# Float32r weights of a hybrid layer: two fixed tiles of four quarters in place of four rotating buffers

## The chip, the cores and the metric

The kernel runs on one core of a Trainium2 chip. The metric is the device time of one execution of the program, in microseconds (us). The engines are named as in the profile: PE is TensorE's matrix multiplication and PEld its loading of weights, DVE is VectorE, ACT is ScalarE, POOL is GpSimd, and SP is the engine that issues most of the DMAs here. SBUF is the on-chip memory that the engines read; an address below is a byte offset within one of its 128 partitions.

## The reference

One layer of an encoder with attention and convolution, for 512 frames of a new stream and 64 frames of a running one (576 in all), with 2048 features:

```python
def hybrid_layer(x, k_past, v_past, conv_past, g_norm1, w_in, g_q, g_k, conv_w,
                 g_attn_out, g_conv_out, w_out, g_norm2, w_gate, w_up, w_down):
    ...
    hn = rmsnorm(x, g_norm1)
    proj = hn @ w_in
    q, k, v, gb, gc, hc = jnp.split(proj, ...)
    ...
    o_attn = stick_breaking_blocks(q, k_all, v_all, P).reshape(B, T, ATTN_W)
    u = gc * hc
    padded = jnp.concatenate([conv_past.astype(u.dtype), u], axis=1)
    conv = (conv_w[0] * padded[:, 0:T] + conv_w[1] * padded[:, 1:T + 1]
            + conv_w[2] * padded[:, 2:T + 2])
    o_conv = gb * conv
    ...
    mix = jnp.concatenate([rmsnorm(o_attn, g_attn_out), rmsnorm(o_conv, g_conv_out)], axis=-1)
    x = x + mix @ w_out
    h2 = rmsnorm(x, g_norm2)
    x = x + (jax.nn.silu(h2 @ w_gate) * (h2 @ w_up)) @ w_down
    return x, k, v, new_conv
```

There are 8 heads of 128 for the attention and 8 groups of 128 channels for the convolution; `w_in` has 6144 columns, `w_out` 2048, `w_gate` and `w_up` 5632 each, and `w_down` has 5632 rows. Everything is float32. Nearly all of the arithmetic is in the five matrix products.

## The kernel before, in words

**How a float32 product is made.** TensorE multiplies in the type float32r, which keeps fewer bits than float32. Each operand is therefore split in two: the high part is a cast to float32r (on ACT), the low part is the operand minus its high part (on DVE). A product is then the sum of three matmuls: high weights by high frames, low weights by high frames, high weights by low frames. These three matmuls of one 128x128 weight block with 288 frames (half of 576) stand one behind the other in the program; the prediction calls them a triple. So the weight operand alternates high, low, high.

**Columns.** Part of the input projection and the whole output projection go column by column. A column is 2048 elements of each partition: 16 weight blocks of 128 columns for `w_in`, 8 blocks of 256 columns for `w_out`. A DMA brings the raw column (`load_weight`), `weight_split` takes the two tiles for its parts, and ACT and DVE fill them in halves of 1024 elements (`weight_parts`, L211). `step` (L301) issues the three matmuls and `product` the whole column. There are 20 such columns of `w_in`, 4 early ones, 10 late ones beside the attention and 6 for the convolution, and 8 of `w_out` (`out_proj`). Raw columns are loaded and split ahead of their use by small generators that the matmul stream advances (`Pipeline.tick`).

**Units.** The rest of the input projection and all of the feed-forward part use units: 2x2 blocks multiplied with seven products instead of eight (Strassen's way, in a form with sums of frames and of weights). A product of a unit is 24 matmuls on a weight operand of 1024 elements (8 weight blocks by three), or fewer in the down projection and in some units of the convolution. `unit_weights` takes a tile for high and low part of such an operand: the low part at the tile's start, the high part from element 1040. A `prepare` function casts and subtracts some products ahead (L310, L311 in the gate, up and down units), and a `multiply` function issues the matmuls: L1181 in the first units, L1534 in the units of the convolution, L2047 in gate, up and down.

**The buffers.** The weight pool has three tags: `raw` (one tile), `whi` and `wlo`, with two buffers each. Each tile of the last two has 2064 elements, 8256 bytes. A column takes the next `whi` buffer for its high part and the next `wlo` buffer for its low part. A unit's product takes one buffer, from `whi` and `wlo` in turn, for both its parts. In the built program the buffers start at bytes 19200 and 27456 (`whi`), 35712 and 43968 (`wlo`).

**The order.** The order of TensorE's instructions is written out by hand for the whole program. Those of ACT, DVE, POOL and SP are set by a scheduler up to the last gate unit but one, SP's in parts by hand, and by hand behind that. In the output projection (L1727 and L1728 multiply the finished PSUM tile and add it to the residual) the DVE order is thus the scheduler's.

Of the kernel before, what the change touches and what calls it, by code (L numbers as in the profile page):

```python
# [11 lines left out]
F32R = mybir.dt.float32r  # L12
# [4 lines left out]
P = 128  # L17
# [50 lines left out]
def down_calls():  # L68

    done, calls, gone = [0] * DC, [], 0  # L70
    for d, a, b in DOWN:
        assert done[d] == a and b <= gone + SLOTS
        done[d] = b
        calls.append([p + SLOTS for p in range(gone, min(done)) if p + SLOTS < NFP])
        gone = min(done)
    assert gone == NFP
    return calls


class TwoParts:  # L80

    def __init__(self, hi, lo):
        self.two = (hi, lo)

    def __getitem__(self, key):
        part, rest = key[1], (key[0], *key[2:])
        if isinstance(part, slice):
            return TwoParts(*(t[rest] for t in self.two[part]))
        return self.two[part][rest]
# [31 lines left out]
def tile_hybrid_stream_step(  # L121
# [6 lines left out]
    nc = tc.nc  # L128
# [12 lines left out]
    wpool = ctx.enter_context(tc.tile_pool(name="wpool", bufs=2, side="left"))  # L141
# [34 lines left out]
    first_out = len(specs)  # L176
# [9 lines left out]

    ready = []
    raw_tile = {"A": wpool.tile([P, 2, 2048], F32, tag="raw", name="raw_a", bufs=1)}

    def weight_tile(tag, name):  # L190
        return wpool.tile([P, 2064], F32R, tag=tag, name=name)[:, :2048]

    def unit_weights(turn):
        t = wpool.tile([P, 2064], F32R, tag=("whi", "wlo")[turn % 2], name="whl")
        return TwoParts(*(t[:, a : a + 1024].rearrange("p (j c) -> p j c", c=P) for a in (1040, 0)))

    def weight_raw(i):
        src, nk, ncol = specs[i]
# [2 lines left out]

    def weight_split(i):
        nk, ncol = specs[i][1:]
        hi = weight_tile("whi", f"whi{i}")[:, : nk * ncol]
        lo = weight_tile("wlo", f"wlo{i}")[:, : nk * ncol]
        ready.append((hi.rearrange("p (k c) -> p k c", k=nk), lo.rearrange("p (k c) -> p k c", k=nk)))
        return hi, lo

    def weight_parts(raw, hi, lo, a, b, lo_eng):
        nc.scalar.copy(out=hi[:, a:b], in_=raw[:, a:b])  # L210
        lo_eng.tensor_tensor(out=lo[:, a:b], in0=raw[:, a:b], in1=hi[:, a:b].bitcast(F32), op=ALU.subtract)  # L211

    raws = {}
# [6 lines left out]
    def split_weight(lo_eng):  # L220
        raw = raws[len(ready)]
        n = specs[len(ready)][1] * specs[len(ready)][2]
        hi, lo = weight_split(len(ready))
        for a in range(0, n, 1024):
            weight_parts(raw, hi, lo, a, a + 1024, lo_eng)
# [255 lines left out]
    with tc.manual_schedule(engines={mybir.EngineType.Activation, mybir.EngineType.DVE, mybir.EngineType.SP}):  # L481
        raw, raw3, src = weight_raw(0)
        raws[0] = raw
        hi, lo = weight_split(0)
# [873 lines left out]
    def load_sum(q, j0=None):  # L1358
        if not j0:
            bt[q] = bt["pool"].tile([P, NP, 2, HALF], F32R, tag=f"t{q}", name=f"xs_t{q}")  # L1360
        j0, j1 = (0, NP) if j0 is None else (j0, j0 + 4)
        nc.sync.dma_start(out=bt[q][:, j0:j1].bitcast(F32), in_=xs_dram[q, j0:j1].rearrange("j f p t -> p j f t"))
# [248 lines left out]
    def load_forms(tile_, at, f):  # L1611
        ft[f] = tile_[:, at : at + NH // 2]
        nc.sync.dma_start(out=ft[f].bitcast(F32), in_=form_dram[f - 1].rearrange("j f p t -> p j f t"))
# [23 lines left out]
    def add_x(d):  # L1637
        nc.gpsimd.dma_start(out=x2t[d], in_=xt_dram[2 * d : 2 * d + 2].rearrange("k p t -> p k t"), accum_op=ALU.add)
# [26 lines left out]
    corder = [(0, 1), (0, 2), (1, 1), (0, 7), (0, 6), (1, 2), (0, 5), (0, 3), (0, 4), (1, 6), (1, 7), (1, 5)]  # L1665
# [17 lines left out]
    for k_, (n, p_) in enumerate(corder):  # L1683
        if (n, p_) == (NCU - 1, 1):
            turn_mode.enter_context(tc.manual_schedule(engines={mybir.EngineType.SP}))
        if k_ == len(begin) - 1:
            start_mode.close()
        conv_run(n, p_)
        for q in begin[k_] if k_ < len(begin) else range(k_ + 4, min(k_ + 5, len(corder))):
            conv_prepare(*corder[q])  # L1690
        if k_ in (0, 2):
            load_sum(3, k_ * 2)
        if n == NCU - 1 and p_ in (6, 7, 4):
            q = {6: 1, 7: 2, 4: 3}[p_]
            t = bt["pool"].tile([P, NH, 2, HALF], F32R, tag=f"t{q}", name=f"forms{q}")
            for at, f in enumerate({1: (1, 2), 2: (6, 7), 3: (5, 3)}[q]):
                load_forms(t, 4 * at, f)
            if p_ == 7:
                load_forms(apool.tile([P, NH // 2, 2, HALF], F32R, tag="oa", name="forms0"), 0, 4)
        if (n, p_) == (NCU - 1, 3):  # L1700
            open_out()
        if n >= NCU and p_ == (3 if n < NCU + 2 or n == len(CU) - 1 else 4):
            add_x(n - NCU)
        if k_ in (len(corder) - 10, len(corder) - 5):
            load_weight()
        if k_ == len(corder) - 4:
            split_weight(nc.vector)

    turn_mode.close()

# [437 lines left out]
    turn = [0]  # L2148
# [252 lines left out]
```

## Time and profile before

| | us |
|---|---|
| median of 3 runs | 2323.15 (2323.01 to 2323.67) |
| the profiled execution | 2322.45 |
| its span, first to last instruction | 2320.7 |

The mean granted clock of TensorE was 0.999. The stages follow one another on TensorE, with the share of the window that each kept TensorE busy, from the windows view of the whole kernel:

| stage | window, us | PE busy | matmuls |
|---|---|---|---|
| start, early columns | 0 to 62 | 59.35 | 432 |
| first units | 62 to 182 | 119.75 | 909 |
| attention, late columns, columns of the convolution | 182 to 455 | 272.43 | 2018 |
| units of the convolution | 455 to 745 | 289.74 | 2194 |
| output projection | 745 to 846 | 101.00 | 768 |
| gate and up units | 846 to 1834 | 987.33 | 7481 |
| down units | 1834 to 2320.7 | 481.00 | 3649 |

In the rows quoted below, a line such as `PE MATMUL psy<-h_s,whl 128*128 128x288 f32 x21` is a run of 21 matmuls into the PSUM tile `psy`, with the frames of tile `h_s` and the weights of tile `whl`, of 128x128 weights and 128x288 frames. L2047 is the line of the kernel. The busy length of a row overlaps the next row's start, because matmuls are pipelined; what a product takes is read from start to start. In the windows view a row holds the window, its length, and then busy time and count for PE and PEld, the granted clock, the busy share of the DMA engines and GB/s.

### The profile page before, as it was taken

Reading aid. Unit: us, or ns where it says so; the run is one execution under the profiler, and the core shown is the slowest. Engines: PE = TensorE matmul, PEld = TensorE weight load, DVE = VectorE, ACT = ScalarE, POOL = GpSimd, SP = SyncE. Lnnn points to the kernel's source line nnn. Section 1 sums busy time; section 2 is a strip of 40 time slices with the busy share of each in tenths; the row PEclk is TensorE's granted clock in tenths of the full one; section 3 lists DMA queues with packets and bytes.
Section 4 is the critical chain, followed back from the end, with each engine's and each line's share of the span. In section 5 each row is a group of like instructions: output and inputs, shape, how many; then the busy total and the mean of one; then the engine's idle time right before and its main releaser. Section 6 shows DMA issues by size and latency. Waiting matters only on the chain.

```text
span 2320.7 us, 43744 instructions
## 1 busy us (share of the span) xinstructions
PE 2310.6 (100%) x17437; PEld 2302.8 (99%) x17437; DVE 1919.7 (83%) x2853; ACT 1161.1 (50%) x2016; POOL 285.3 (12%) x394
## 2 busy tenths in 40 slices
PE   9999999999999999999999999999999999999999
PEld 9999999999999999999999999999999999999999
DVE  8977887888877899888888888888888777887886
ACT  7535887444455564444444444444444444444444
POOL 2002343111111210000000000000000001431121
PEclk9999999999999999999999999999999999999999
DMA  8776554953389454543544444444344936886543
GB/s 278 214 205 166 154 155 107 345 190 109 107 278 248 145 166 145 160 153 122 155 139 141 150 135 150 133 146 156 114 156 143 357 111 223 223 230 203 195 125 107
DMA packets 584869, 402.54 MB, mean 173 GB/s; under 512 B 91870, under 2 KB 571864, under 8 KB 584664
## 3 DMA queue, kind: packets, MB, share of 16 engines
q1 hardware_dynamic: 574136, 378.56, 52.3%
q0 software_dynamic: 10160, 20.94, 4.0%
q8 instruction: 136, 2.23, 0.4%
q14 instruction: 69, 0.57, 0.1%
q10 hardware_dynamic: 368, 0.24, 0.0%
HBM read 303.53 MB, written 96.16 MB: 172 GB/s over the span
## 4 chain that ended last, share of the span: by engine, by line
PE 88%; DVE 6%; DMA 2%; SPq 2%; issue 1%; ACT 1%; POOL 0%; ACTq 0%; DVEq 0%
PE psy L2047 34%; PE psw L2047 17%; PE psx L2047 8%; PE pj L301 8%; PE psy L1534 7%; PE psw L1534 3%; PE psy L1181 3%; PE psx L1534 2%; PE psw L1181 1%; PE psx L1181 1%; DMA raw_a<-in_w_in_dram 1%; SPq L2244 1%; DMA raw_b<-in_w_down_dram 1%; DVE whl L311 1%; DVE wlo L211 1%
## 5 line engine op out<-in xcount | busy, mean ns | idle before, releaser
L2047 PE MATMUL psy<-h_s,whl 128*128 128x288 f32 x2787 | 410.6, 294 | 0.0
L2047 PEld LDWEIGHTS psy<-h_s,whl 128*128 128x128 f32 x2787 | 382.5, 188 | 0.0
L311 DVE TENSOR_TENSOR whl<-raw_a,whl 128x1024 fp32r<-128x1024 f32 (+4 forms) x296 | 318.2, 1076 | 54.8 <-ACT whl L310 53.6
L2047 PE MATMUL psw<-t,whl 128*128 128x288 f32 x2400 | 346.9, 295 | 0.0
L2047 PEld LDWEIGHTS psw<-t,whl 128*128 128x128 f32 x2400 | 326.9, 188 | 0.2 <-DVE whl L311 0.2
L310 ACT CAST whl<-raw_a 128x1024 fp32r<-128x1024 f32 (+4 forms) x296 | 267.6, 906 | 103.8 <-issue 35.3
L301 PE MATMUL pj<-x,whi 128*128 128x288 f32 x1248 | 272.6, 299 | 0.1
L311 DVE TENSOR_TENSOR whl<-raw_b,whl 128x1024 fp32r<-128x1024 f32 (+5 forms) x190 | 198.9, 1047 | 66.1 <-ACT whl L310 65.0
L310 ACT CAST whl<-raw_b 128x1024 fp32r<-128x1024 f32 (+5 forms) x190 | 165.1, 871 | 166.5 <-issue 72.3
L2057 ACT COPY part<-psy 128x288 f32<-128x288 f32 x242 | 96.3, 398 | 277.9 <-PE psy L2047 275.7
L301 PEld LDWEIGHTS pj<-x,whi 128*128 128x128 f32 x1248 | 207.4, 189 | 0.8 <-DVE x L464 0.3
L301 PE MATMUL pj<-x,wlo 128*128 128x288 f32 x624 | 184.1, 295 | 0.0
L2047 PE MATMUL psy<-t2t,whl 128*128 128x288 f32 x1212 | 182.9, 294 | 0.0
L2047 PE MATMUL psy<-b22m,whl 128*128 128x288 f32 x1212 | 182.7, 294 | 0.0
L2047 PE MATMUL psx<-h_s,whl 128*128 128x288 f32 x1185 | 173.1, 294 | 0.0
L2047 PEld LDWEIGHTS psy<-t2t,whl 128*128 128x128 f32 x1212 | 167.8, 188 | 0.3 <-DVE whl L311 0.3
L2047 PEld LDWEIGHTS psy<-b22m,whl 128*128 128x128 f32 x1212 | 167.7, 188 | 0.0
L2047 PEld LDWEIGHTS psx<-h_s,whl 128*128 128x128 f32 x1185 | 162.2, 188 | 0.0
L310 ACT CAST whl<-s 128x1024 fp32r<-128x1024 f32 (+5 forms) x81 | 72.2, 891 | 98.5 <-PE psw L2047 98.5
L1826 POOL DMA_DIRECT2D hid_dram<-form x3 | 2.3, 752 | 968.9 <-DVE form L311 967.7
L301 PEld LDWEIGHTS pj<-x,wlo 128*128 128x128 f32 x624 | 117.7, 189 | 0.4
L2047 PE MATMUL psy<-t,whl 128*128 128x288 f32 x576 | 106.8, 295 | 1.3 <-ACT part L2057 1.3
(535 smaller groups left out, 4550.9 us busy)
## 6 DMA issues: line engine op xcount, KB each, us to landing
hid_dram<-form SPq DMA_DIRECT2D x147, 288.0 KB, 2.2
raw_a<-in_w_in_dram SPq DMA_DIRECT2D x31, 1024.0 KB, 5.5
raw_a<-in_w_gate_dram SPq DMA_DIRECT2D x22, 1024.0 KB, 5.4
raw_a<-in_w_up_dram SPq DMA_DIRECT2D x22, 1024.0 KB, 5.6
raw_b<-in_w_gate_dram SPq DMA_DIRECT2D x22, 1024.0 KB, 6.6
raw_b<-in_w_up_dram SPq DMA_DIRECT2D x22, 1024.0 KB, 6.4
h_s<-hid_dram SPq DMA_DIRECT2D x10, 2016.0 KB, 11.9
raw_a<-in_w_out_dram SPq DMA_DIRECT2D x16, 1024.0 KB, 5.5
```

Of the source, the lines that this page charges most:

```text
L211: lo_eng.tensor_tensor(out=lo[:, a:b], in0=raw[:, a:b], in1=hi[:, a:b].bitcast(F32), op=ALU.subtract)
L301: mm(ps, w_[:, k, csl], x_, start=(k == 0 and n == 0), stop=(k == nk - 1 and n == 2))
L310: nc.scalar.copy(out=hi, in_=src)
L311: (lo_eng or nc.vector).tensor_tensor(out=lo, in0=src, in1=hi.bitcast(F32), op=ALU.subtract)
L1181: mm(ps, whl[:, w_, j, :], x_, start=(start and j == 0 and q == 0), stop=(j == NP - 1 and q == 2), skip_group_check=True)
L1534: mm(ps, whl[:, w_, j, :], x_, start=(start and j == 0 and q == 0), stop=(j == m - 1 and q == 2), skip_group_check=True)
L1826: q.dma_start(out=hid_dram[fp][2 * n - 2 : 2 * n].rearrange("f p t -> p f t"), in_=t.bitcast(F32))
L2047: mm(ps, whl[:, w_, j, :], x_, start=(start and j == 0 and q == 0), stop=(j == len(xs_) - 1 and q == 2), skip_group_check=True)
L2057: nc.scalar.copy(out=t, in_=st["y"])
L2244: nc.sync.dma_start(out=y[g : g + t1 - t0, b0 : b0 + 32].rearrange("(b t) c -> t b c", t=32), in_=ap[32 * q : 32 * (q + 1), t0:t1].rearran ...
```

## The change

`whi` and `wlo` become two fixed tiles with one buffer each: `low_all` of 4096 elements and `high_all` of 4160, with four quarters of 1024 elements each (those of `high_all` start at element 16). The bytes of both together are the same as those of the four buffers. `quarter` hands out the quarters in a ring: a unit's product takes one, with its high part in `high_all` and its low part in `low_all`; a column takes two, and `Halves` indexes the two as one. In the built program `low_all` starts at byte 19200 and `high_all` at 35584. The split of the first output column is written as two halves, one product of the convolution apart, instead of one call.

```diff
--- before.py
+++ after.py
@@ -77,6 +77,19 @@
     return calls
 
 
+class Halves:
+
+    def __init__(self, parts, size):
+        self.parts, self.size = parts, size
+
+    def __getitem__(self, key):
+        i = key[1]
+        half = ((i.start or 0) if isinstance(i, slice) else i) // self.size
+        off = half * self.size
+        i = slice((i.start or 0) - off, i.stop - off) if isinstance(i, slice) else i - off
+        return self.parts[half][(key[0], i, *key[2:])]
+
+
 class TwoParts:
 
     def __init__(self, hi, lo):
@@ -186,13 +199,18 @@
 
     ready = []
     raw_tile = {"A": wpool.tile([P, 2, 2048], F32, tag="raw", name="raw_a", bufs=1)}
-
-    def weight_tile(tag, name):
-        return wpool.tile([P, 2064], F32R, tag=tag, name=name)[:, :2048]
+    low_all = wpool.tile([P, 4096], F32R, tag="wlo", name="low_all", bufs=1)
+    high_all = wpool.tile([P, 4160], F32R, tag="whi", name="high_all", bufs=1)
+    ring = [0]
+
+    def quarter():
+        a = ring[0] % 4
+        ring[0] += 1
+        b = 16 + a * 1024
+        return high_all[:, b : b + 1024], low_all[:, a * 1024 : a * 1024 + 1024]
 
     def unit_weights(turn):
-        t = wpool.tile([P, 2064], F32R, tag=("whi", "wlo")[turn % 2], name="whl")
-        return TwoParts(*(t[:, a : a + 1024].rearrange("p (j c) -> p j c", c=P) for a in (1040, 0)))
+        return TwoParts(*(t.rearrange("p (j c) -> p j c", c=P) for t in quarter()))
 
     def weight_raw(i):
         src, nk, ncol = specs[i]
@@ -201,10 +219,10 @@
 
     def weight_split(i):
         nk, ncol = specs[i][1:]
-        hi = weight_tile("whi", f"whi{i}")[:, : nk * ncol]
-        lo = weight_tile("wlo", f"wlo{i}")[:, : nk * ncol]
-        ready.append((hi.rearrange("p (k c) -> p k c", k=nk), lo.rearrange("p (k c) -> p k c", k=nk)))
-        return hi, lo
+        assert nk * ncol == 2048
+        two = list(zip(quarter(), quarter()))
+        ready.append(tuple(Halves([t.rearrange("p (k c) -> p k c", c=ncol) for t in part], nk // 2) for part in two))
+        return tuple(Halves(part, 1024) for part in two)
 
     def weight_parts(raw, hi, lo, a, b, lo_eng):
         nc.scalar.copy(out=hi[:, a:b], in_=raw[:, a:b])
@@ -1704,7 +1722,10 @@
         if k_ in (len(corder) - 10, len(corder) - 5):
             load_weight()
         if k_ == len(corder) - 4:
-            split_weight(nc.vector)
+            first_split = weight_split(first_out)
+            weight_parts(raws[first_out], *first_split, 0, 1024, nc.vector)
+        if k_ == len(corder) - 3:
+            weight_parts(raws[first_out], *first_split, 1024, 2048, nc.vector)
 
     turn_mode.close()
 
```

TensorE's and POOL's rows are the same as before, one for one, apart from the names of the weight tiles. The orders that a scheduler makes of ACT, DVE and SP differ in a few stretches at the end of the convolution's units and in the output projection. Two of them follow.

The first is DVE in the output projection, in the fourth column. `low_all<-raw_a,high_all` (before: `wlo<-raw_a,whi`) is the subtraction that makes a low part for a coming column, `po<-pjo,R_c` the multiply that empties a PSUM tile of a finished product, and `x_3` a block of the residual; `h_s` and `b` are operands of the feed-forward part. Before:

```order
L1727 TENSOR_TENSOR po<-pjo,R_c 128x288
L1728 TENSOR_TENSOR x_3_7946<-po,x_3_7946 128x288
L1776 SCALAR_TENSOR_TENSOR h_s_8998<-x_3_7946,vec,h_s_8998 128x288
L1727 TENSOR_TENSOR po<-pjo,R_c 128x288
L1728 TENSOR_TENSOR x_3_7946<-po,x_3_7946 128x288
L211 TENSOR_TENSOR wlo_9631<-raw_a,whi_9630 128x1024 x2
L1776 SCALAR_TENSOR_TENSOR b_9621<-x_3_7946,vec,b_9621 128x288
```

Of the change:

```order
L1748 TENSOR_TENSOR po<-pjo,R_c 128x288
L1749 TENSOR_TENSOR x_3_7806<-po,x_3_7806 128x288
L1797 SCALAR_TENSOR_TENSOR h_s_8804<-x_3_7806,vec,h_s_8804 128x288
L229 TENSOR_TENSOR low_all<-raw_a,high_all 128x1024
L1748 TENSOR_TENSOR po<-pjo,R_c 128x288
L229 TENSOR_TENSOR low_all<-raw_a,high_all 128x1024
L1749 TENSOR_TENSOR x_3_7806<-po,x_3_7806 128x288
L1748 TENSOR_TENSOR po<-pjo,R_c 128x288
L1797 SCALAR_TENSOR_TENSOR b_9419<-x_3_7806,vec,b_9419 128x288
```

Before, both subtractions stand behind the second multiply shown and its addition. Now the first of them stands ahead of that multiply, and the second between it and its addition, so both are issued ahead of where they were.

The second is SP at the same stage. `raw_a<-in_w_out_dram` loads a raw column of `w_out`; `b_dram` and `x_dram` receive operands and residuals for later. Before:

```order
L218 DMA raw_a<-in_w_out_dram 128x8x256
L1780 DMA b_dram<-b_9299 128x288
L1786 DMA x_dram<-x_2_7945 128x2x576
L1780 DMA b_dram<-b_9460 128x288
L218 DMA raw_a<-in_w_out_dram 128x8x256
L1780 DMA b_dram<-b_9460 128x288
```

Of the change:

```order
L236 DMA raw_a<-in_w_out_dram 128x8x256
L1801 DMA b_dram<-b_9101 128x288 x2
L1807 DMA x_dram<-x_1_7804 128x2x576
L1807 DMA x_dram<-x_2_7805 128x2x576
L1801 DMA b_dram<-b_9260 128x288 x2
L236 DMA raw_a<-in_w_out_dram 128x8x256 x2
```

The second load of a column stood between two stores of one operand; now it stands behind both, and the next load follows it at once.

## The prediction

> **What bounds the kernel now.** I read the page first, then the list of waits, then TensorE's timeline. From the page:
>
> ```profile
> span 2320.7 us, 43744 instructions
> PE 2310.6 (100%) x17437; PEld 2302.8 (99%) x17437; DVE 1919.7 (83%) x2853; ACT 1161.1 (50%) x2016; POOL 285.3 (12%) x394
> PE 88%; DVE 6%; DMA 2%; SPq 2%; issue 1%; ACT 1%; POOL 0%; ACTq 0%; DVEq 0%
> ```
>
> TensorE is never free, and the chain that ended last is 88% TensorE. The waits say the same; these are the two longest of TensorE's list (who waited, for whom, us in total, times, longest):
>
> ```profile
> PE psy L2047 <- ACT part L2057: 1.3, 2, 1.0
> PE warm L491 <- DVE acA L327: 1.1, 1, 1.1
> ```
>
> So buffers, queues and the other engines cost nearly nothing now, and an edit of the weight tiles can move the time in two ways only: by making TensorE wait, or by changing how long one matmul keeps it. For the second I read the timeline of TensorE (start in us, length, engine, line, operation, tiles, count). One product of a gate or up unit is 24 matmuls on one weight tile; a row may hold 24, or 21 and 3, because the moving operand has two names:
>
> ```profile
> 846.00 2.93 PE L2047 MATMUL psy<-h_s,whl 128*128 128x288 f32 x21
> ...
> 1002.91 3.31 PE L2047 MATMUL psw<-t,whl 128*128 128x288 f32 x24
> 1006.06 2.95 PE L2047 MATMUL psx<-h_s,whl 128*128 128x288 f32 x21
> 1008.84 0.56 PE L2047 MATMUL psx<-h_z,whl 128*128 128x288 f32 x3
> 1009.24 2.95 PE L2047 MATMUL psy<-t2t,whl 128*128 128x288 f32 x21
> 1012.03 0.56 PE L2047 MATMUL psy<-t2z,whl 128*128 128x288 f32 x3
> 1012.42 3.31 PE L2047 MATMUL psw<-t,whl 128*128 128x288 f32 x24
> 1015.57 0.56 PE L2047 MATMUL psy<-h_z,whl 128*128 128x288 f32 x3
> ...
> 1819.48 3.34 PE L2047 MATMUL psw<-t,whl 128*128 128x288 f32 x24
> ```
>
> From start to start the four products take 3.15, 3.18, 3.18 and 3.15 us with nothing waited for. They are the same arithmetic on the same shapes; what differs is the buffer. In the built program the four weight buffers start at bytes 19200, 27456, 35712 and 43968, which is 0, 64, 128 and 192 modulo 256, and a unit's high part lies 64 bytes further in that count than its low part. The product at 1002.91 reads the buffer at 0, that at 1006.06 the one at 192, then 64, then 128, then 0 again. Over the 305 products of 24 between the first and the last row shown that wait for nothing, the start times put them at 3148 ns (0), 3177 (64), 3149 (128) and 3186 (192), each buffer within 4 ns in nearly all of its 75 to 77 products. The mean is 3165 ns, or 395.6 ns for one **triple** (high, low and again high weights, the unit of the sum below); the buffer at 0 makes 393.5. Neither ACT, DVE nor the DMAs show in this, or the times would scatter.
>
> The first units and the convolution's units show the same spread:
>
> ```profile
> 102.32 3.35 PE L1181 MATMUL psw<-xf,whl 128*128 128x288 f32 x24
> 105.51 3.34 PE L1181 MATMUL psy<-xf,whl 128*128 128x288 f32 x24
> 108.68 6.46 PE L1181 MATMUL psy<-x,whl 128*128 128x288 f32 x48
> 114.98 3.35 PE L1181 MATMUL psw<-xf,whl 128*128 128x288 f32 x24
> ...
> 525.26 3.33 PE L1534 MATMUL psx<-x,whl 128*128 128x288 f32 x24
> 528.43 3.31 PE L1534 MATMUL psy<-xs_t,whl 128*128 128x288 f32 x24
> 531.58 3.35 PE L1534 MATMUL psw<-xs_t,whl 128*128 128x288 f32 x24
> 534.77 9.66 PE L1534 MATMUL psy<-x,whl 128*128 128x288 f32 x72
> ```
>
> 3.19, 3.17 and twice 3.15 us (48 in 6.30) in the first; 3.17, 3.15 and 3.19 in the second.
>
> In the columns, high and low parts lie in two tiles, so the pairs of residues are others. There the low row marks the triple:
>
> ```profile
> 58.12 0.29 PE L301 MATMUL pj<-x,wlo 128*128 128x288 f32 x1
> 69.53 0.29 PE L301 MATMUL pj<-x,wlo 128*128 128x288 f32 x1
> 416.88 0.30 PE L301 MATMUL pj<-x,wlo 128*128 128x288 f32 x1
> 429.22 0.30 PE L301 MATMUL pj<-x,wlo 128*128 128x288 f32 x1
> 429.62 0.30 PE L301 MATMUL pj<-x,wlo 128*128 128x288 f32 x1
> 441.60 0.30 PE L301 MATMUL pj<-x,wlo 128*128 128x288 f32 x1
> ```
>
> 29 triples lie between the first two (high at 64, low at 192): 393.4 ns each. 31 between the next two (0 and 192): 398.1. 30 between the last two (64 and 128): 399.3. The output projection alternates between two pairs, one column of 96 matmuls from row to row:
>
> ```profile
> 744.64 0.30 PE L301 MATMUL pjo<-mixm,whi 128*128 128x288 f32 x1
> 757.40 0.30 PE L301 MATMUL pjo<-mixm,whi 128*128 128x288 f32 x1
> 770.00 0.29 PE L301 MATMUL pjo<-mixm,whi 128*128 128x288 f32 x1
> 782.74 0.29 PE L301 MATMUL pjo<-mixm,whi 128*128 128x288 f32 x1
> ```
>
> 12.76 us (0 and 128), 12.60 (64 and 192), 12.74 (0 and 128).
>
> **The change part by part.** *Where the weights lie.* In the changed program the low tile starts at 19200 and the high one at 35584, both multiples of 256, so every low part is at 0 and every high part at 64: the residues that the buffer at 0 has today, at every quarter alike (quarters are 4096 bytes apart). Moving operands and PSUM tiles keep their addresses, and TensorE's order is the same row for row. I therefore give every triple the 393.5 ns of that buffer. How many there are, from the windows view of one line each (us of the window, TensorE's busy time and count):
>
> ```profile
> 62.00:182.00 120.00, 111.20 (x840) 110.86 (x840) 1.00 0.71 202
> 455.00:745.00 290.00, 289.33 (x2184) 288.58 (x2184) 1.00 0.62 188
> 846.00:1834.00 988.00, 986.70 (x7475) 985.90 (x7476) 1.00 0.48 152
> 1834.00:2310.00 476.00, 474.14 (x3578) 471.84 (x3577) 1.00 0.62 187
> ```
>
> These are the first units (L1181), the convolution's (L1534), gate and up, and down (both L2047). Gate and up: 7475 / 3 = 2492 triples by 2.1 ns, **5.2 us**. First and convolution units: 1008 triples by 2.2 (their four mean 3.17 us as well), **2.2 us**. Down: products there have 9 to 18 matmuls; 476.00 us over 3578 matmuls is 133 ns with its transposes and waits, near the 131.9 of gate and up, so I take the same 2.1 ns for 1193 triples, **2.5 us**, with 1.0 as the low end since short products meet a border between buffers more often. Sixteen later columns have 512 triples at a mean of 398.7: by 5.2 ns, **2.7 us**; of the four early ones half are at 398 already, 64 triples, 0.3. Output projection: half of eight columns, 0.15 us each, **0.6 us**. That makes 13.5 us.
>
> One term is a choice. A product's first step to the low weights and its last step border on another buffer. In the buffer at 0 the step high to low takes 130.2 ns inside a product, but 133.2 as its first step, where the matmul before used weights at 192; its last step takes 133.5 against 131.2 inside (from the starts of the single matmuls of some 180 products on that buffer, of which the rows at 1002.91 and 1015.57 are two). In the ring the neighbour is at 64 too. If the border then costs what the inside costs, each of some 700 products of all units gains up to 5 ns more, 3.7 us in all; if it is the border itself that costs, nothing. I take 1 us, nearer to nothing, since a border of equal residues stands in no row. **Sum: 14.5 us less.**
>
> *Waits.* Four buffers of 1024 + 1024 become four quarters of the same, so the ring releases a unit's quarter by the same matmul as now, the low part one matmul earlier. Two steps are later: the high part of the second half of the first two columns behind the first units waits for 24 matmuls more, one product, 3.2 us. Behind that cast ACT holds its next activations, but the first reader of that half still stands 73 matmuls (9.6 us) behind the release, where the cast and subtraction need about 2.3 us; I put it at nothing, at most 3.2 us. In the output projection a half is released while the column still runs, and DVE's two subtractions move ahead of the last product's multiply, as the rows above show, half of them earlier by 12 to 24 matmuls. That multiply then starts one subtraction later:
>
> ```profile
> 771.48 2.35 DVE L211 TENSOR_TENSOR wlo<-raw_a,whi 128x1024 fp32r<-128x1024 f32 x2
> ```
>
> About 1.2 us, covered by the three PSUM buffers of the projection (a product takes 24 matmuls, 3.2 us); TensorE waits for none of it now, so the gain is nil and the loss under 0.5 us. SP's weight loads move ahead of or behind a store or two; their users stand some 100 matmuls (13 us) off: nothing. The two halves of the first output weights are split one product apart, both beside TensorE's work: nothing.
>
> *A rule against it.* The Trainium skill ("TensorE: Matmul & The Clock Gate", section "Step-by-step: what each phase is for") says TensorE has two independent read ports and "Loading the next tile's weights doesn't steal SBUF read bandwidth from the running matmul." By that rule the weights' address would not matter and the sum would be zero, 2323 us. The trace does not agree: 3.15 against 3.18 us by buffer, with nothing else different.
>
> **The rivals.** *Place, not residue.* The four rates could belong to the buffers' whole addresses. Then four quarters at new places mix again and the mean stays: 2323 us, give or take 3. For it: each residue occurs at one place only. Against it: the buffer at 0 gives 3148 ns with five different moving operands at very different addresses, and columns at 64/192 run at 393.4 both with x and in the projection.
>
> *Distance, and slower.* High and low of one unit are 4,160 bytes apart now and 16,448 in the new tiles. If the alternation over that distance costs what the worst pairs cost today, 398.5 ns a triple, units lose 2.9 ns by 4693 triples and the fast columns 5 ns by 190: plus 14.5 us, 2338. It turns slower as soon as a triple exceeds 396.2. Against it: the columns have high and low 16,512 bytes apart, and those at 64/192 belong to the fastest.
>
> *A new wait.* The two later casts, or the last product's multiply, reach TensorE: up to 5 us given back, 2312 to 2316.
>
> That the change doesn't put the weights where it says is excluded by the built addresses.
>
> **How the numbers follow.** The profiled execution took 2322.45 us (span 2320.7 and 1.75 around it), 0.7 under the median of 2323.15; minus 14.5 it would be 2308.0, and against the median 2308.7, **2309** in round numbers. Forecast 0.78 (2305 to 2312, its own range: 1.0 for down at the low end, 3 us for borders at the other); new wait 0.05; place 0.11; distance 0.06. The range 2305 to 2319 holds the first two and the better edge of the third, and leaves out under 2 in 10. About 0.2%, 4.6 us, is what a measurement of this kernel can tell from no change: faster 0.83, same 0.11, slower 0.06.
>
> **What would show it.** Right: in gate and up every product of 24 takes one time, 3.14 to 3.15 us, whatever its quarter; each column of the projection 12.6 us; late columns 393 to 394 ns a triple; the waits of TensorE as short as now. Wrong by place: products still alternate. Wrong by distance: all of them alike, and above 3.17. Wrong by waits: a new line of over 2 us in TensorE's list, at about 190 us (ACT) or between 745 and 846 (DVE).

## The result, and the profile after

The change takes 2313.58 us (median of 5 runs, 2313.21 to 2317.67); the kernel before, run beside it, 2323.67 (2323.01 to 2326.17). The ratio is 0.9964, with a 95% interval of 0.9952 to 0.9975. Against 2323.15 us, the median that the prediction starts from, that is 9.6 us less, where the prediction's sum was 14.5: inside the range, and outside the forecast's own 2305 to 2312. The profiled execution of the change is the longest of the five, 2317.67 us.

The page of the change:

```profile
span 2316.0 us, 43740 instructions
PE 2302.8 (99%) x17437; PEld 2292.8 (99%) x17437; DVE 1918.5 (83%) x2853; ACT 1161.5 (50%) x2016; POOL 282.3 (12%) x394
PE 89%; DVE 5%; DMA 3%; ACT 1%; issue 1%; SPq 0%; POOL 0%; ACTq 0%; DVEq 0%
```

TensorE's waits (who waited, for whom, us, times, longest):

```profile
PE ss L635 <- ACT b22m L328: 2.0, 1, 2.0
PE warm L509 <- DVE acA L345: 1.1, 1, 1.1
PE pjo L319 <- DVE po L1748: 1.0, 2, 0.5
```

Before the change, the sums of squares (`ss`) had this line, and the list had none for `pjo`:

```profile
PE ss L618 <- DVE b22m L311: 0.5, 1, 0.5
```

TensorE is busy 7.8 us less, but the span is only 4.7 us shorter. The waits for the sums of squares have grown from 0.5 us to 2.0 and, in a smaller line, 0.3, and one wait is new, in the output projection, for the multiply that empties a PSUM tile.

The rate itself did what was forecast. These rows of TensorE's timeline of the change are the first matmuls of four gate and up products in a row and of a product near the end of the stage, and then two low rows of a late column:

```profile
1005.33 0.29 PE L2068 MATMUL psw<-t,high_all 128*128 128x288 f32 x1
...
1008.47 0.30 PE L2068 MATMUL psx<-h_s,high_all 128*128 128x288 f32 x1
...
1011.62 0.29 PE L2068 MATMUL psy<-t2t,high_all 128*128 128x288 f32 x1
...
1014.77 0.29 PE L2068 MATMUL psw<-t,high_all 128*128 128x288 f32 x1
...
1817.16 0.29 PE L2068 MATMUL psw<-t,high_all 128*128 128x288 f32 x1
...
414.28 0.29 PE L319 MATMUL pj<-x,low_all 128*128 128x288 f32 x1
...
426.47 0.29 PE L319 MATMUL pj<-x,low_all 128*128 128x288 f32 x1
```

3.14, 3.15 and 3.15 us from product to product, whatever the quarter. From the first of these rows to the fifth are 811.83 us; the same two products lay 816.57 us apart before (1002.91 and 1819.48). Between the last two rows lie 31 triples of the late column, at 393.2 ns each, where those at 0 and 192 took 398.1.

So the missing part must be waits. The starts of the same matmuls, taken from the traces, divide the span into stages (us, from the stage's first matmul to that of the next; e1, e6 and e12 are runs below, e6 is the change once more):

| stage | before | change | e6 | e1 | e12 |
|---|---|---|---|---|---|
| start, early columns (432 matmuls) | 60.92 | 60.45 | 62.07 | 60.06 | 61.74 |
| first units | 117.55 | 116.71 | 116.67 | 117.10 | 116.68 |
| attention, late columns | 275.53 | 273.75 | 273.75 | 273.76 | 273.78 |
| units of the convolution | 289.51 | 288.40 | 287.50 | 287.49 | 287.55 |
| output projection | 101.36 | 104.12 | 102.09 | 100.69 | 100.69 |
| two gate products, sums of squares | 7.57 | 10.51 | 10.35 | 9.46 | 7.46 |
| the next three products | 9.77 | 11.80 | 9.70 | 10.92 | 11.28 |
| gate and up, the rest | 969.22 | 963.35 | 963.78 | 963.36 | 963.51 |
| down, to the last matmul | 483.76 | 480.59 | 479.87 | 479.32 | 479.88 |

Three rows go the wrong way, all between 740 and 867 us: the projection (3.4 us over e1), the sums of squares (2.9 over before) and the three products behind them (2.0). The start differs by up to 2 us between these executions (60.06 to 62.07 us), and that much must be allowed for between single runs. The convolution's units take 0.9 us more in this execution of the change than in e6, the same kernel, so that too differs between executions.

**In the projection** the wait begins on SP. Its issues before the change (start, length with the wait, what):

```profile
797.13 0.36 SPq L1786 DMA_DIRECT2D x_dram<-x  x1
798.24 0.33 SPq L1780 DMA_DIRECT2D b_dram<-b  x1
799.40 0.37 SPq L218 DMA_DIRECT2D raw_a<-in_w_out_dram  x1
```

and after:

```profile
787.04 11.99 SPq L236 DMA_DIRECT2D raw_a<-in_w_out_dram  x2
799.58 0.89 SPq L1801 DMA_DIRECT2D b_dram<-b  x2
800.57 0.43 SPq L1807 DMA_DIRECT2D x_dram<-x  x1
```

The store of the residual (`x_dram`) used to be issued ahead of the stores of `b` and of the next load. Now it stands behind them. What this holds up is told by the chain of waits of the change in that stretch (start, length, what):

```profile
800.57 6.37 DMA x_dram<-x
807.36 0.43 ACT t L328
807.79 0.44 ACT h_s L1796
808.56 0.95 ACT high_all L228
809.53 1.23 DVE low_all L229
...
812.18 0.46 DVE x L1749
```

ACT's cast of the frame sums `t` is written over the residual that the store reads, so it waits for the store to land. Behind it on ACT stand the next operand and the weights' casts, behind those DVE's subtraction, and behind that the multiply for which TensorE waits. ACT's list of waits in the projection has it in one line in the change:

```profile
ACT t L328 <- DMA x_dram<-x: 9.0, 5, 3.9
```

Before the change there is no such line.

**At the end of the projection** DVE comes late to the last multiply. Its timeline in the change (start, length, line, operation; in brackets the idle time ahead of it and what ended it):

```profile
849.35 1.43 DVE L329 TENSOR_TENSOR low_all<-raw_a,high_all 128x1024 fp32r<-128x1024 f32 x1 [1.29 <-ACT high_all L328]
850.70 0.45 DVE L1748 TENSOR_TENSOR po<-pjo,R_c 128x288 f32<-128x288 f32 x1
...
851.43 0.45 DVE L1749 TENSOR_TENSOR x<-po,x 128x288 f32<-128x288 f32 x1
...
852.94 0.45 DVE L1786 TENSOR_TENSOR acc<-acc,sq 128x288 f32<-128x288 f32 x1
...
854.16 0.45 DVE L329 TENSOR_TENSOR b22m<-acc,b22m 128x288 fp32r<-128x288 f32 x1
```

Before the change the two stood the other way round:

```profile
847.40 0.45 DVE L1727 TENSOR_TENSOR po<-pjo,R_c 128x288 f32<-128x288 f32 x1
...
849.59 1.23 DVE L311 TENSOR_TENSOR whl<-raw_a,whl 128x1024 fp32r<-128x1024 f32 x1
```

In the change the projection's last matmul started at 844.2 us, but its multiply only at 850.70, 6.5 us later; before the change 1.5 us lay between the two (845.87 and 847.40). Ahead of the multiply stands now the subtraction for a later gate product, which first waited 1.29 us for its cast. The squares, their sum and its split (`b22m`) follow, and the sums of squares on TensorE wait for the split. Behind that wait the granted clock is half for some 5 us (window, then busy time and count of PE, PEld, DVE, ACT and POOL, granted clock, DMA share, GB/s):

```profile
852.00:854.00 2.00, 0.06 (x1) 0.07 (x1) 2.00 (x4) 1.88 (x5) 0.00 (x0) 0.86 0.63 246
854.00:856.00 2.00, 1.88 (x6) 1.56 (x7) 2.00 (x4) 0.43 (x1) 0.00 (x0) 0.50 0.56 201
...
862.00:864.00 2.00, 2.00 (x18) 2.00 (x17) 2.00 (x3) 1.94 (x4) 0.00 (x0) 1.00 0.79 282
```

21 matmuls took 240 ns each in place of 131, 2.3 us.

### The profile page after: what moved, and what is told of

It reads as the page before. It is cut to its first block, busy times and chain, and to the rows that moved or that the text cites. A ratio compares the mean times of both kernels' runs of the same rounds, so it can differ in the third digit from the quotient of the medians.

```text
span 2316.0 us, 43740 instructions
## 1 busy us (share of the span) xinstructions
PE 2302.8 (99%) x17437; PEld 2292.8 (99%) x17437; DVE 1918.5 (83%) x2853; ACT 1161.5 (50%) x2016; POOL 282.3 (12%) x394
## 4 chain that ended last, share of the span: by engine, by line
PE 89%; DVE 5%; DMA 3%; ACT 1%; issue 1%; SPq 0%; POOL 0%; ACTq 0%; DVEq 0%
PE psy L2068 35%; PE psw L2068 18%; PE psx L2068 9%; PE pj L319 7%; PE psy L1552 6%; PE psw L1552 3%; PE psy L1199 3%; PE psx L1552 2%; PE psw L1199 1%; DMA x_dram<-x 1%; PE psx L1199 1%; PE pjo L319 1%; PE po L1085 0%; PE z L957 0%; DVE x L482 0%
## 5 line engine op out<-in xcount | busy, mean ns | idle before, releaser
L2068 PE MATMUL psy<-h_s,high_all 128*128 128x288 f32 x1858 | 410.7, 295 | 0.1
L329 DVE TENSOR_TENSOR low_all<-raw_a,high_all 128x1024 fp32r<-128x1024 f32 (+4 forms) x296 | 316.8, 1070 | 57.5 <-ACT high_all L328 56.6
L2068 PE MATMUL psw<-t,high_all 128*128 128x288 f32 x1600 | 344.9, 294 | 0.0
L328 ACT CAST high_all<-raw_a 128x1024 fp32r<-128x1024 f32 (+4 forms) x296 | 267.4, 905 | 102.9 <-issue 36.8
L2068 PEld LDWEIGHTS psy<-h_s,high_all 128*128 128x128 f32 x1858 | 313.2, 189 | 0.3 <-ACT t L328 0.3
L2068 PE MATMUL psy<-h_s,low_all 128*128 128x288 f32 x929 | 274.3, 295 | 0.0
L319 PE MATMUL pj<-x,high_all 128*128 128x288 f32 x1248 | 270.3, 297 | 0.2 <-DVE x L482 0.2
L2068 PEld LDWEIGHTS psw<-t,high_all 128*128 128x128 f32 x1600 | 265.5, 188 | 0.0
L2068 PE MATMUL psw<-t,low_all 128*128 128x288 f32 x800 | 235.3, 294 | 0.0
L319 PEld LDWEIGHTS pj<-x,high_all 128*128 128x128 f32 x1248 | 206.5, 188 | 1.2 <-DVE x L482 0.4
```

What stands on the lines that cost most here:

```text
L319: mm(ps, w_[:, k, csl], x_, start=(k == 0 and n == 0), stop=(k == nk - 1 and n == 2))
L328: nc.scalar.copy(out=hi, in_=src)
L329: (lo_eng or nc.vector).tensor_tensor(out=lo, in0=src, in1=hi.bitcast(F32), op=ALU.subtract)
L2068: mm(ps, whl[:, w_, j, :], x_, start=(start and j == 0 and q == 0), stop=(j == len(xs_) - 1 and q == 2), skip_group_check=True)
```

## The experiments

e1 to e4 ran on one chip with one set of runs of the kernel before (2321.54 us), e5 to e8 on another occasion (2323.03), e9 to e11 (2321.48) and e12 (2321.02) on two more. So ratios are compared across occasions, and times within one.

### e1: the old order in the projection, the new addresses

```diff
     def split_weight(lo_eng):
         raw = raws[len(ready)]
         n = specs[len(ready)][1] * specs[len(ready)][2]
+        if len(ready) > first_out:
+            a = ring[0] % 4 * 1024
+            weight_split(len(ready))
+            hi, lo = high_all[:, 16 + a : 16 + a + n], low_all[:, a : a + n]
+            weight_parts(raw, hi, lo, 0, n, lo_eng)
+            return
```

> Output columns 2 to 8 are split by one cast and one subtraction of 2048 elements, so a split waits for the whole column ahead of it, as it did with a buffer of its own. That brings the rows of DVE and SP in the output projection back to those of before, up to the last column; the weights stay at residues 0 and 64. Theory A (the new order, which follows from a release by halves, makes the waits): the waits of TensorE for the multiply L1748 go, the projection takes 100.8 us from its first matmul to the first gate unit (104.1 in the change), and the time falls by about 3, to 2310 to 2311. Theory B (TensorE is faster and DVE has become the bound of this stage whatever its order): the waits stay and so does the time, 2313 to 2314.

2310.35 us (2309.44 to 2311.96), ratio 0.9953 (0.9941 to 0.9966). The projection takes 100.69 us, and TensorE's list has no wait for the multiply. It has this one:

```profile
PE ss L641 <- ACT b22m L334: 1.7, 1, 1.7
```

Theory A holds. DVE has the same work here and TensorE the same rate as in the change, and the waits are gone, so the stage isn't bound by DVE whatever its order (theory B). But the edit changed the rows of DVE and of SP together; e3 separates them.

### e2: the first split in one piece

```diff
-            first_split = weight_split(first_out)
-            weight_parts(raws[first_out], *first_split, 0, 1024, nc.vector)
-        if k_ == len(corder) - 3:
-            weight_parts(raws[first_out], *first_split, 1024, 2048, nc.vector)
+            split_weight(nc.vector)
```

> The split of the first output column is one call at its old place again; all else as in the change. Theories A and B both put it at nothing: 2313.2 to 2313.8, with the same waits in the projection. If the split in two pieces sets off the late rows of DVE and SP, the waits shrink and the time falls by up to 3 us.

Here the second quarter is written ahead of the product that still reads it, so the third last product of the convolution is computed with other weights; the instructions are the change's. 2314.35 us (2313.30 to 2315.46), ratio 0.9968; the projection 102.73 us, the sums 10.35. Nothing is gained, as expected, so this run also stands for the change on e1's occasion: 4.0 us over e1, with ranges that don't overlap.

### e3: the store first, DVE's subtractions ahead of the multiply as in the change

```diff
     def after_b2(kt):
         j = kt // 2
+        if kt % 2:
+            nc.sync.dma_start(out=x2_dram[kt - 1 : kt + 1].rearrange("k p t -> p k t"), in_=x2t[j])
...
         if kt % 2:
-            nc.sync.dma_start(out=x2_dram[kt - 1 : kt + 1].rearrange("k p t -> p k t"), in_=x2t[j])
             pipe.spawn(frame_sums(j), 2)
```

> The store of the residual (x_dram, on SP) stands ahead of the two stores of the operand b again, as before the change; DVE's subtractions stay ahead of the last product's multiply. Theory A1 (the late store holds ACT's casts of the frame sums, which hold the weights' casts behind them): ACT's waits for the store, 9.0 us in the change, go, TensorE's waits in the projection go with them, and the time falls to about 2310. Theory A2 (DVE's own order is the cause): TensorE still waits about 3 us in the projection and the time stays at 2313 to 2314.

2310.88 us (2310.50 to 2314.11), ratio 0.9958 (0.9945 to 0.9972). The projection takes 100.77 us, as in e1. ACT's wait for the store in the projection:

```profile
ACT t L328 <- DMA x_dram<-x: 2.7, 3, 1.0
```

The wait has shrunk from 9.0 us, and TensorE's list has no wait for the multiply, although the first subtraction of each column still stands ahead of it. So it was the store (A1), and DVE's order alone costs next to nothing in this execution (against A2). The edit let the scheduler move a few other rows of ACT and DVE too, so the store is not the only difference. The size of this wait and the time of the projection go together over these traces: none and 100.69 (e1), 2.7 and 100.77 (e3), 6.2 and 102.09 (e6), 9.0 and 104.12 (the change). But e9 below, with the order of e3 in the projection but for a few rows, has

```profile
ACT t L328 <- DMA x_dram<-x: 4.5, 4, 1.8
PE pjo L319 <- DVE po L1748: 0.5, 1, 0.5
```

and takes 102.11 us there. A store issued at about 821 us took 5.04 us to land, against 3.50 in e3. So the early store is not safe in every execution, and where it lands late, the subtractions ahead of the multiply add to it; which part each has isn't separated. With e1's order ACT's list has no wait for the store (e1, e10, e12), and the projection takes 100.69 us each time. The sums of squares still wait 2.0 us in e3.

### e4: a written order from the last column on

```diff
     def ahead():
         load_columns([("A", 0), ("A", 1)])
+        tail.enter_context(tc.manual_schedule(engines={mybir.EngineType.Activation, mybir.EngineType.DVE}))
...
     for k_ in range(2, AHEAD):
         prepare(*order[k_])
+    tail.close()
```

on top of e1.

> As e1, and ACT and DVE follow the written order from the last output column to the split of the fourth gate product, so that the last product's multiply and the sums of squares stand ahead of the next weights' subtractions. Theory A, with the wait for the sums of squares at 852 us (3.0 us, and the half clock behind it, 2.5 us more) put down to the subtraction ahead of the last multiply: both go, and the time is the forecast's, 2308.5 to 2310, with little between runs. If that wait has another cause (the store of the last residual, say), it stays and the time is that of e1.

2312.14 us (2311.90 to 2314.01), ratio 0.9961: by the medians 1.8 us over e1, and over the range expected. The wait for the sums is gone (6.83 us for that stage), and no run of 240 ns matmuls follows. New ones have come, of the gate products for their weights and in the projection's last column:

```profile
PE psy L2074 <- DVE low_all L335: 2.8, 2, 1.6
PE pjo L325 <- DVE po L1754: 0.9, 1, 0.9
```

So the order made the wait for the sums; but an order that puts all weights behind the sums only moves the wait.

### e5: the store first, and a written order from the last multiply on

```diff
                 nc.vector.tensor_tensor(out=x2(kt)[:, a:b], in0=t, in1=x2(kt)[:, a:b], op=ALU.add)
+                if c == D // 256 - 1 and n == 3:
+                    last_work()
...
+    def last_work():
...
+        sums_parts(0)
+        prepare(*order[2])
...
+    prepare(*order[3])
+    sums_parts(1)
```

on top of e3, with ACT and DVE in written order from that multiply to the last row.

> As e3 (the store of the residual first), and ACT and DVE follow a written order from the last product's multiply of the output projection to the split of the fourth gate product: multiply, residual, first sum of squares, third product's weights, then the rest, with the fourth product's weights and the second sum of squares last. Theory A (the 2.0 us wait for the sums of squares comes from the third product's subtraction standing ahead of that multiply, and the half clock comes from the wait): the wait shrinks to 0.3 us as before the change, no matmul behind it takes 240 ns, and no product waits for its weights as in e4; against e3 that is 2.9 + 1.0 us, so 2306 to 2307.5. Rival: the chain from the last PSUM tile to the sums is as long in any order; then 1.5 us or more of the wait stays, and the time is over 2309.

The first half's sum is split here without the last of its 16 squares, so one thing that the split otherwise waits for is missing. 2309.81 us (2309.49 to 2312.07), ratio 0.9946. The stage of the sums takes 9.10 us, 1.4 less than in e3 and 1.5 more than before the change, and 14 matmuls of 240 ns follow. A miss for theory A. The time is the rival's, but TensorE's waits for the sums, 1.1 and 0.2 us, are less than the rival's 1.5; the order and the missing square may both have a share in that. DVE still reached the last multiply 3.1 us after the projection's last product, and so the sums stayed late.

### e6: the change again

No edit.

> The change itself once more, beside e5 on one chip. 2312.5 to 2314.5; the projection 102.5 to 104.2 us, a wait of about 2 us for the sums of squares, and some twenty matmuls of 240 ns behind it.

2314.29 us (2313.59 to 2315.26), ratio 0.9964 (0.9950 to 0.9977). Projection and sums as expected, but no half clock: the steps from matmul to matmul around the sums are those of the change's first trace (0.63, 2.37 and 0.73 us from start to start), yet the next matmuls took 131 ns.

### e7, e8, e11: other residues, same order

```diff
-        b = 16 + a * 1024
+        b = 32 + a * 1024
```

with 0 in e8 and 48 in e11.

> One number: the high tile's quarters start at element 32 in place of 16, so high parts lie at 128 and low parts at 0 modulo 256; distance, order and places stay. If the residue pair sets the rate, every triple takes the 398.3 ns that the columns with the pair 0 and 128 took before the change: units 3.19 us a product, some 5500 triples slower by 4.9 ns, 2338 to 2342. If the ring itself (one tile, quarters 4096 bytes apart) made the gain, 3.15 us a product and 2313 stay.

> The high tile's quarters start at element 0: high and low parts both at 0 modulo 256. No run so far has this pair. By the residue theory all products take one time, whatever it is, between 3.15 (2313) and 3.19 us (2341); if equal residues hurt as 0 and 128 do, the upper end. If the ring made the gain, 3.15 us.

> The high quarters start at element 48: 192 and 0 modulo 256. With the pairs so far (64 and 0: 393.4 ns a triple, 0 and 0: 396.7, 128 and 0: 400.0) a triple would cost 396.7 or more if the distance of the residues sets it (192 is as far from 0 as 64, the other way round), so 2331 or more; 393.4 and 2313 if only being 64 apart matters. One rate for all products in either case.

One run each: 2347.63, 2331.68 and 2342.28 us. The two products named above, in TensorE's timeline of e7:

```profile
1014.69 0.30 PE L2068 MATMUL psw<-t,high_all 128*128 128x288 f32 x1
...
1840.29 0.30 PE L2068 MATMUL psw<-t,high_all 128*128 128x288 f32 x1
```

of e8:

```profile
1009.00 0.29 PE L2068 MATMUL psw<-t,high_all 128*128 128x288 f32 x1
...
1827.72 0.29 PE L2068 MATMUL psw<-t,high_all 128*128 128x288 f32 x1
```

and of e11:

```profile
1011.62 0.29 PE L2068 MATMUL psw<-t,high_all 128*128 128x288 f32 x1
...
1837.22 0.29 PE L2068 MATMUL psw<-t,high_all 128*128 128x288 f32 x1
```

825.60, 818.72 and 825.60 us for the same 6192 matmuls that take 811.83 in the change: 400.0, 396.7 and 400.0 ns a triple against 393.3. One number in an index, with every instruction in its old place, puts the kernel 17 to 33 us over e6, whose five runs lie within 1.7 us; the ring made no gain of its own. Two details missed. The pair of 128 and 0 costs 400.0, not the 398.3 of its mirror. And in e11 the rate isn't one: the first units, the output projection, the down units and most of the convolution's units run at 397.8 a triple, the last columns of `w_in` and gate and up at 400.0, so there something beside the two residues counts, and what it is stays open.

These runs also bear on the wait in the projection, since the order is the change's. ACT waits for the store 5.5 us in e7 and 5.9 in e11, but the projection takes 102.40 and 101.83 us, which is 256 triples at 400.0 and 397.8 ns and nothing more. In these two executions the late store thus cost TensorE nothing, where 6.2 us of the same wait cost 1.4 in e6: the order makes ACT's wait, and how much of it reaches TensorE seems to depend on TensorE's own rate too. No run tests that alone.

### e9, e10: the sums of squares one product later

```diff
+    rest = []
...
         if p_ == 1:
             ...
             multiply(st["y"], n, 1, True)
+            if n == 1:
+                rest.pop()()
...
         elif p_ == 2:
             ...
             multiply(x, n, 2, True)
+            def scale():
+                row_scale2()
+                done(0, 0, x, st["p1"])
+
             if n == 0:
-                row_scale2()
-            add(0, 0, x, st["p1"])
-            done(0, 0, x, st["p1"])
+                rest.append(scale)
+            else:
+                add(0, 0, x, st["p1"])
+                done(0, 0, x, st["p1"])
```

on top of e3 (e9) and of e1 (e10).

> As e3, and TensorE makes the sums of squares (ss, with the scale R2 behind them) one gate product later, behind the third instead of the second. Theory A (two waits outside the weights' addresses hold the change back: the late store in the projection, and the sums of squares, which DVE and ACT finish some 3 us too late): both are gone, with the half clock behind the second; the sums wait 0.3 us or less, and of e3's time 2.9 + 0.7 us go: 2306 to 2308. Rival: the wait moves on to the next user (the scale R2, or a PSUM tile that is kept longer), and the time stays at 2310 or more.

> As e1 (output columns split whole), with the sums of squares one product later as in e9. By theory A the same time as e9 within 0.7 us, 2306 to 2308, since e1 and e3 leave the same projection (100.7 and 100.8 us). If DVE's order in the projection matters beyond the store, it is faster than e9 by 1 us or more.

2315.69 and 2314.52 us, ratios 0.9974 and 0.9972: the rival, and worse than it said. The sums wait no more, but the next product's PSUM tile is the one that held them, and it is read (`ms`, on ACT) late. In e9:

```profile
PE psx L2069 <- ACT ms L619: 6.7, 1, 6.7
```

In its chain of waits, `ms` at 858.86 stands behind a weights' cast on ACT, and that one behind three sums of weights on DVE. By the medians e10 is 1.2 us under e9, and its projection takes 100.69 us against 102.11: this is the case that e10's last sentence names, so e1's order in the projection is worth something beyond moving the store.

### e12: the old order in the projection and a written one at its end

```diff
+                if kt == KD - 1 and i == 1:
+                    tail.enter_context(tc.manual_schedule(engines={mybir.EngineType.Activation, mybir.EngineType.DVE}))
...
                 nc.vector.tensor_tensor(out=x2(kt)[:, a:b], in0=t, in1=x2(kt)[:, a:b], op=ALU.add)
+                if kt == KD - 1 and i == 1:
+                    prepare(*order[2])
...
         parts2.append((sh, sl))
+    prepare(*order[3])
+    tail.close()
```

on top of e1; the two calls replace those behind.

> As e1 (output columns split whole), with ACT and DVE in a written order only from the last product's multiply of the projection on: multiply, residual, the third gate product's weights, the last squares, both splits of the sums, then the fourth product's weights. Nothing is left out of the computation. Theory A (the wait for the sums of squares, 2.7 us in e1, is the third product's subtraction and the stall of DVE in front of it, standing ahead of the last multiply): the wait falls to 0.3 to 1.0 us, the half clock behind it goes with it, and the time is 2306.5 to 2308.5. Rival (DVE reaches the end of the projection too late in any order): 1.5 us or more of the wait stays, with the half clock, and the time is 2309.5 or more.

2309.86 us (2308.08 to 2310.95), ratio 0.9947 (0.9934 to 0.9961). TensorE's waits:

```profile
PE psw L2080 <- DVE low_all L335: 1.5, 1, 1.5
...
PE ss L642 <- DVE b22m L335: 0.3, 1, 0.3
```

The sums wait 0.3 us, their stage takes 7.46 us, and no half clock follows: theory A, as to the cause. But 1.5 us come back two products later, where DVE is behind with the weights, and so the time is 1.4 us above the expected range (it is the rival's time, without the rival's wait). Of the kernels that compute everything, this one has the lowest ratio; between it and e1 the runs can't decide (the intervals overlap). e1 is 4.0 us under e2, which stands for the change on its occasion. e12 has no such partner: its ratio, 0.9947 against 0.9964 of the change, says about 4 us too, but the two intervals overlap.

## Why the prediction was right in sign and short by a third

**What bounds the kernel, and the rates: right.** Every product of 24 takes 3.15 us whatever its quarter. The terms, from the table's columns without the new waits: first and convolution units 2.9 us (2.2 forecast), projection 0.7 (0.6), gate and up 5.9 (5.2 and most of the 1.0 for borders), down 4.4 in e1, of which 1.3 are two waits for `part` that stand in the list of before and not in e1's, so 3.1 (2.5). Late columns were over-sized: 1.8 us in place of 2.7. The 0.3 of the early ones can't be seen beside the spread of the start. In all 14.4 us, against 14.5.

**Borders.** From the first to the last of the products shown, a triple gained 4.74 us / 2064 = 2.3 ns, where the buffer at 0 gave 2.1. The 0.2 ns make 1.5 ns a product, so a border between equal residues seems a little cheaper, by about a third of the 5 ns that stood as the upper end.

**What the prediction drew from a rule on two read ports: rightly rejected.** By the Trainium skill ("TensorE: Matmul & The Clock Gate", "Step-by-step: what each phase is for") loading the next weights takes no read bandwidth from the running matmul. The prediction took from it, as a rival, that the weights' address would not matter. e7 and e8 changed nothing but that address and took 400.0 and 396.7 ns a triple against 393.3, so it does matter. Whether the running matmul or the loading of the weights becomes slower, no run shows.

**Waits: this is the step that failed.** The prediction said of SP: "SP's weight loads move ahead of or behind a store or two; their users stand some 100 matmuls (13 us) off: nothing." It asked for the users of the loads, and not for those of the store that now stood behind them. That user, the cast of `t` on ACT, waits for the store at once; the projection lost 1.4 us in e6 and 3.4 in the first trace. e3, whose edit moves the store alone, took it all back, and e9, with the same edit, lost 1.4 again; e1's order lost nothing. Of DVE it said that a multiply one subtraction later is "covered by the three PSUM buffers", a loss under 0.5 us. Within the projection that held where the store came in time (e3). At its end it didn't: the last multiply feeds no buffer but the sums of squares, two products ahead of their use. There the subtraction and the idle time in front of it cost 2.8 to 2.9 us, and half clock behind it up to 2.3 more; e12 takes the wait back by another order of ACT and DVE alone.

**The size.** 1.4 us in the projection and 2.8 at the sums, as in e6, are 4.2 us, and the median misses the forecast by 4.6. The execution profiled first had more of each and the half clock, 8.3 us, and took 4.1 us more than the median.

**The rivals.** Place and distance are out by the rates. A new wait had a chance of 0.05, and a price of up to 5 us, 2312 to 2316; it is what happened, on top of the full gain. It named the places (the two later casts, the last product's multiply), but not SP's store, which starts the one in the projection. That the time lies inside the range is owed to a range that held this rival too, not to the forecast. The sign that the prediction named, a line of over 2 us in TensorE's list, does not show either: the list of the change has 1.0 us for the projection, where the starts of the matmuls, read against e1, give 3.4.

## What to carry to other kernels

When a matmul stream alternates between two weight operands and nothing waits, list its start-to-start times by the operands' addresses; here one offset, which moves the residues and nothing else, was worth up to 1.7% of a triple's time. When an edit releases buffers in smaller pieces, a scheduler may move work on several queues, here DVE's, ACT's and SP's: follow each moved store to who overwrites its source, and each moved DVE row to the last user of the stage, not only to the steady state. The output projection, in which DVE is busy for 88.01 of 101.00 us (745 to 846 us before the change), has little room for a wait in front of DVE's queue, and pushing one wait away at its end brought up the next (e4, e9, e12).

## What the runs showed of the hardware

The time of a triple of 128x288 float32r matmuls goes with the residues modulo 256 of the two alternating weight parts: 393.3 ns with 64 and 0 (high, low), 396.7 with 0 and 0, 400.0 with 128 and 0, in units and projection alike. With 192 and 0 it is 397.8 or 400.0 by the stage (e11), so the pair doesn't always settle it. That 256 is the modulus isn't shown. 128 is too small: 64 and 0 took 393.3, and 64 and 128 took 399.3 before the change. A larger one is not excluded: the new quarters and the old buffer at 0, which share a rate, also agree modulo 4096 (low part at 2816, high part at 2880).

After a step of 2.0 to 2.4 us from one matmul's start to the next, at the sums of squares, the granted clock was half for 9 to 21 matmuls in the change, e1, e2, e3, e7, e8 and e11, and not at all in e6, with the same step. After 1.5 us it was half in e5 (14 matmuls) and not in e4, and not after 1.9 us in e4 or 1.8 in e12, at later products. After 7.1 and 6.4 us, in e9 and e10, it was half for 18 and 13. The Trainium skill ("TensorE: Matmul & The Clock Gate", "Part 1: The HAM clock gate (the "warmup" mystery)") gives half clock after an idle window of some 3.4 us that runs free of the program. That one kernel does either fits a window that runs free; that 1.5 to 2.4 us can be enough does not fit its length, unless the short idle times around it count.
